# A column sum over 256 MB: eight running rows on VectorE in place of a fold and a TensorE sum for every load

## The chip, the cores and the metric

The kernel runs on one NeuronCore of a Trainium2 chip. A core has TensorE (matrix products, results in PSUM), VectorE (called DVE in a profile), ScalarE (ACT), GpSimd (POOL) and SyncE (SP), each with an instruction queue of its own that is worked off in order. Here SP issues all loads from HBM into SBUF. Every transfer is cut into pieces that 16 DMA engines carry side by side. The engines wait for each other and for transfers through semaphores.

The metric is the time of one execution on the device in microseconds.

## What is computed

```python
def setup_inputs():
    batch, seq, dim = 32, 1024, 2048
    return {"grad_output": np.random.randn(batch, seq, dim).astype(np.float32)}

def reference(grad_output):
    return np.sum(grad_output, axis=(0, 1)).astype(np.float32)
```

The gradient of a bias: 32,768 vectors of 2048 floats are added up to one. That is 268.4 MB read once, and 8 KB written.

## The kernel before

The input is taken as 32,768 lines of 2048 floats. What is called a row below is 128 such lines, one in each of SBUF's 128 partitions: a tile of 128x2048 floats, 1 MB (1,048,576 bytes). There are 256 rows. A load brings several rows at once; those of one partition lie one behind the other in HBM.

**Buffers.** One tile, `ring`, has three slots (`SLOTS`) of eight rows (`M`), 64 KB in each partition. `UNITS` lists the loads: 29 of eight rows, then 6, 4, 3, 3, 3, 2, 2. Unit i goes to slot i % 3. The last two units leave out the last 256 columns (`B`) of their rows, and behind them come one more row without these columns and five small loads of 256 columns, `late`, for the columns left out.

**A unit's way.** SP issues its load (`load`, L113). VectorE waits until it has landed (`take`) and folds it to two rows in place (`fold`, L69): rows 4 to 7 are added to rows 0 to 3, a 128x8192 add, then rows 2 and 3 to rows 0 and 1, a 128x4096 add. TensorE then adds the two rows over the partitions (`sums`, L95): a matmul with a column of ones in place of weights, for four quarters of the 2048 columns in four column groups of the array, summed up in the PSUM tile `acc`. In a profile a row's sums are eight records. When both rows are summed, TensorE raises `s_free`, and SP, which waits for it, issues the load that reuses the slot. So unit i alone decides when load i+3 is issued.

TensorE also computes filler products into the tile `junk` (L158, `FILL` = 3, 0, 2 for the three slots) that nobody reads.

**Order.** All semaphores are written out by hand within `tile_critical`. VectorE's 27 first units are a loop on its own queue (9 rounds of three slots), and TensorE's 36 units are one of 12 rounds.

**The end.** After the last units TensorE sums the late row into `acc` and the five late pieces into a second PSUM tile, `accr` (L174). ScalarE copies `acc` to SBUF (`res`, L188). The second half of the columns lies in two PSUM partitions in alternating blocks of 128; ScalarE and VectorE each put one of them in order (`joint`, L192). VectorE adds `accr` to the last 256 columns (L197). Four stores write the result: SP the first 1024 columns (L201), ScalarE the joint ones (L205), and SP and ScalarE 128 each of the last 256 (L208).

Of the kernel before, what the change touches and what calls it, by code (L numbers as in the profile page):

```python
# [7 lines left out]
P = 128  # L8
M = 8
SLOTS = 3  # L10
LOOPS = 9
UNITS = (M,) * 29 + (6, 4, 3, 3, 3, 2, 2)
B = 256
LATE = 5
FILL = (3, 0, 2)


@with_exitstack
def kernel(
# [10 lines left out]

    nc = tc.nc
    f32 = mybir.dt.float32
    D = out.shape[-1]
    flat = grad_output.rearrange("b s d -> (b s) d")
    Q = D // 4
    H = B // 2
    W = M * D  # L40
    add = mybir.AluOpType.add
    C = D - B

    sb = ctx.enter_context(tc.tile_pool(name="sb", bufs=1))
    ps = ctx.enter_context(tc.tile_pool(name="ps", bufs=1, space=bass.MemoryType.PSUM))
    ring = sb.tile([P, SLOTS * W], f32, name="ring")
    ones = sb.tile([P, 1], f32, name="ones")
    fill = sb.tile([P, 512], f32, name="fill")
    res = sb.tile([P, Q], f32, name="res")
    joint = sb.tile([P, C - 2 * Q], f32, name="joint")  # L50
    acc = ps.tile([P, 512], f32, name="acc")
    accr = ps.tile([P, 512], f32, name="accr")
    junk = ps.tile([P, 512], f32, name="junk")

    some = lambda name, n: [tc.alloc_semaphore(f"{name}{k}") for k in range(n)]
    landed, red, late = some("landed", SLOTS), some("red", SLOTS), some("late", 1 + LATE)
    s_one, s_free, s_vec, s_left, s_right, s_res, s_end, s_last, s_out = (
        tc.alloc_semaphore(n)
        for n in ("one", "free", "vec", "left", "right", "res", "end", "last", "out")
    )  # L60
    q, v, t, a, p = nc.sync, nc.vector, nc.tensor, nc.scalar, nc.gpsimd

    def take(engine, sem, n):
        engine.wait_ge(sem, n)
        engine.sem_inc(sem, -n)  # L65

    def fold(at, n, by):
        part = ring[:, at : at + n * D]
        return v.tensor_tensor(  # L69
            out=part, in0=part, in1=ring[:, at + by * D : at + (by + n) * D], op=add  # L70
        )

    def unit(i):

        s, m = i % SLOTS, UNITS[i]
        at = s * W
        take(v, landed[s], 16)
        steps = {8: ((4, 4), (2, 2)), 6: ((2, 4), (2, 2)), 4: ((2, 2),), 3: ((1, 2),), 2: ()}[m]
        for k, (n, by) in enumerate(steps):
            if k:  # L80
                take(v, s_vec, 1)
            fold(at, n, by).then_inc(red[s] if k + 1 == len(steps) else s_vec, 1)
        if not steps:
            v.sem_inc(red[s], 1)

    def shares(x):


        ends = x[:, 2 * Q :].rearrange("p (b g c) -> p g b c", g=2, c=H)
        return [x[:, :Q], x[:, Q : 2 * Q], ends[:, 0], ends[:, 1]]  # L90

    def sums(at, w=D):
        for g, x in enumerate(shares(ring[:, at : at + w])):
            o = acc[32 * g : 32 * g + 1, : Q if g < 2 else (w - 2 * Q) // 2]
            mm = t.matmul(  # L95
                o if g < 2 else o.rearrange("p (b c) -> p b c", c=H),
                lhsT=ones[:],
                rhs=x,
                start=False,
                stop=False,  # L100
                tile_position=(0, 32 * g),
                skip_group_check=True,
            )
        return mm

    with tc.tile_critical(sync_engine=mybir.EngineType.Pool):

        def load(at, m, row, c0, w, sem):
            part = ring[:, at : at + m * D].rearrange("p (m d) -> p m d", m=m)[:, :, c0 : c0 + w]
            src = flat[row * P : (row + m) * P].rearrange("(p m) d -> p m d", p=P)[:, :, c0 : c0 + w]  # L110
            if w == D:
                part, src = (x.rearrange("p m d -> p (m d)") for x in (part, src))
            q.dma_start(out=part, in_=src).then_inc(sem, 16)  # L113

        row = 0
        for i, m in enumerate(UNITS):
            if i >= SLOTS:
                q.wait_ge(s_free, i - SLOTS + 1)
            load(i % SLOTS * W, m, row, 0, D if i + 2 < len(UNITS) else C, landed[i % SLOTS])
            row += m  # L120

        end = (len(UNITS) - 1) % SLOTS * W
        load(end + 2 * D, 1, row, 0, C, late[0])
        ends = [(end + 3 * D + k * B) for k in range(LATE)]
        row -= LATE - 1
        for at, m in zip(ends[::2], (2, 2, 1)):
            part = flat[row * P : (row + m) * P].rearrange("(p m) d -> p m d", p=P)
            for j in range(m):
                k = ends.index(at) + j
                q.dma_start(  # L130
                    out=ring[:, at + j * B : at + (j + 1) * B], in_=part[:, j, C:]
                ).then_inc(late[1 + k], 16)
            row += m


        v.memset(ones[:], 1.0).then_inc(s_one, 1)  # L136
        v.memset(fill[:], 0.0).then_inc(s_one, 1)  # L137
        v.memset(acc[:], 0.0).then_inc(s_one, 1)  # L138
        v.memset(accr[:], 0.0).then_inc(s_one, 1)  # L139
        with v.Fori(0, LOOPS) as _:  # L140
            for s in range(SLOTS):
                unit(s)
        for i in range(LOOPS * SLOTS, len(UNITS)):
            if i + 2 >= len(UNITS):
                at = i % SLOTS * W
                v.wait_ge(s_free, i - SLOTS + 1)
                v.memset(  # L147
                    ring[:, at : at + 2 * D].rearrange("p (m d) -> p m d", m=2)[:, :, C:], 0.0
                ).then_inc(s_vec, 1)
                take(v, s_vec, 1)  # L150
            unit(i)


        t.wait_ge(s_one, 4)
        with t.Fori(0, len(UNITS) // SLOTS) as _:
            for s in range(SLOTS):
                for _ in range(FILL[s]):
                    t.matmul(  # L158
                        junk[0:1, :],
                        lhsT=ones[:],  # L160
                        rhs=fill[:],
                        start=True,
                        stop=True,
                        tile_position=(0, 0),
                    )
                take(t, red[s], 1)
                sums(s * W)
                sums(s * W + D).then_inc(s_free, 1)
        t.wait_ge(late[0], 16)
        sums(end + 2 * D, C).then_inc(s_left, 1)  # L170
        for k, at in enumerate(ends):
            t.wait_ge(late[1 + k], 16)
            for g in (2, 3):
                mm = t.matmul(  # L174
                    accr[32 * g : 32 * g + 1, :H],
                    lhsT=ones[:],
                    rhs=ring[:, at + (g - 2) * H : at + (g - 1) * H],
                    start=False,
                    stop=False,
                    tile_position=(0, 32 * g),  # L180
                    skip_group_check=True,
                )
        mm.then_inc(s_right, 1)

        a.wait_ge(s_left, 1)
        a.copy(out=res[0:97, :], in_=acc[0:97, :]).then_inc(s_res, 1)  # L188
        left = joint[64:65, :].rearrange("p (b g c) -> p g b c", g=2, c=H)
        for g, copy in enumerate((a.copy, v.tensor_copy)):  # L190
            (a, v)[g].wait_ge(s_res, 1)
            copy(  # L192
                out=left[:, g],
                in_=res[64 + 32 * g : 65 + 32 * g, : Q - H].rearrange("p (b c) -> p b c", c=H),
            ).then_inc(s_end, 1)
        v.wait_ge(s_right, 1)
        v.tensor_tensor(  # L197
            out=res[64:97, Q - H :], in0=res[64:97, Q - H :], in1=accr[64:97, :H], op=add
        ).then_inc(s_last, 1)
        q.wait_ge(s_res, 1)  # L200
        q.dma_start(  # L201
            out=out[: 2 * Q].rearrange("(g c) -> g c", g=2), in_=res[0:33:32, :]
        ).then_inc(s_out, 16)
        a.wait_ge(s_end, 2)
        a.dma_start(out=out[None, 2 * Q : C], in_=joint[64:65, :]).then_inc(s_out, 16)  # L205
        for g, e in enumerate((q, a)):
            e.wait_ge(s_last, 1)
            e.dma_start(  # L208
                out=out[None, C + g * H : C + (g + 1) * H],
                in_=res[64 + 32 * g : 65 + 32 * g, Q - H :],  # L210
            ).then_inc(s_out, 16)
        p.wait_ge(s_out, 64)


# [1 line left out]
_INS = ['grad_output']  # L216
_OUTS = [((2048,), 'float32')]
# [25 lines left out]
```

## Time and profile before

| | us |
|---|---|
| three runs: median (lowest to highest) | 629.33 (629.27 to 629.43) |
| profiled execution, its own time | 629.16 |
| its span, first to last instruction | 627.4 |
| VectorE busy | 403.8 (64%), 72 instructions |
| TensorE busy | 188.6 (30%), 724 records |
| of these the filler products | 72.4, 120 records |
| bytes read | 268.44 MB, 428 GB/s over the span |

The span begins with the first instruction of the kernel and ends with the last; the execution's own time also has what lies before and after. A line of the groups gives the source line, the engine, the operation, what is written from what, the shape, the count; behind the first bar the busy time in all and the mean of one in ns; behind the second the time that the engine stood idle before them and what ended it. A line of the timeline gives start and duration in us. Where it shows several instructions merged, as two adds of a unit, the duration goes from the first start to the last end.

### The profile page before, as it was taken

To read this page: it belongs to the slowest core of one execution; us is meant where nothing else is said; L and a number is where in the kernel's file an instruction comes from. 1 tells how busy PE (TensorE), PEld (TensorE's weight loads), DVE (VectorE), ACT (ScalarE), POOL (GpSimd) and SP (SyncE) were. 2 spreads that over 40 slices of the span, in tenths; PEclk is the share of its full clock that TensorE was granted. 3 is DMA by queue.
4 is the path that set the end of the run, shared out by engine and by line. 5 is a ranking of instruction groups with operands and counts; after the bars stand their busy time and mean duration, and the time that the engine had idled before them with its cause. 6 is when DMAs were issued, how large, how long until landed. Compare 5 with 4: busy or idle time off the path is not lost. (4 is left out here: it accounts for less than half of the span.)

```text
span 627.4 us, 1778 instructions
## 1 busy us (share of the span) xinstructions
PE 188.6 (30%) x724; PEld 29.1 (5%) x724; DVE 403.8 (64%) x72; ACT 2.4 (0%) x3; POOL 0.2 (0%) x4
## 2 busy tenths in 40 slices
PE   3023222342034231323420342214233213421776
PEld 0000000000000000000000000000000000000111
DVE  0566786667866668766687666786666866668732
ACT  0000000000000000000000000000000000000000
POOL 0000000000000000000000000000000000000000
PEclk8565576756577656766566766577665767665879
DMA  9999999999999999999999999999999999999997
GB/s 401 401 468 401 468 401 468 401 468 401 468 401 468 401 464 405 464 405 460 409 455 414 447 422 439 430 430 439 422 447 414 455 409 460 405 447 418 429 422 285
DMA packets 6314, 268.45 MB, mean 428 GB/s; under 512 B 677, under 2 KB 1319, under 8 KB 1962
## 3 DMA queue, kind: packets, MB, share of 16 engines
q1 hardware_dynamic: 6310, 268.44, 99.1%
q10 hardware_dynamic: 4, 0.00, 0.0%
HBM read 268.44 MB, written 0.01 MB: 428 GB/s over the span
## 5 line engine op out<-in xcount | busy, mean ns | idle before, releaser
L69 DVE TENSOR_TENSOR ring<-ring 128x8192 f32<-128x8192 f32 (+2 forms) x64 | 400.5, 6258 | 210.0 <-DVEq L65 205.6
L95 PE MATMUL acc<-ring,ones 128*1 128x512 f32 (+1 forms) x584 | 121.3, 969 | 432.5 <-PEq L65 432.4
L158 PE MATMUL junk<-fill,ones 128*1 128x512 f32 x120 | 72.4, 744 | 2.9 <-DVE accr L139 2.9
L95 PEld LDWEIGHTS acc<-ring,ones 128*1 128x1 f32 x584 | 15.4, 100 | 519.7 <-issue 518.7
L158 PEld LDWEIGHTS junk<-fill,ones 128*1 128x1 f32 x120 | 13.1, 110 | 73.8 <-issue 73.8
L192 DVE COPY joint<-res 1x384 f32<-1x384 f32 x1 | 0.5, 547 | 7.6 <-ACT res L188 7.6
L188 ACT COPY res<-acc 97x512 f32<-97x512 f32 x1 | 0.6, 586 | 620.8 <-PE acc L95 620.8
L147 DVE MEMSET ring<- 128x512 f32 x2 | 1.0, 485 | 1.8 <-PE acc L95 1.8
L174 PE MATMUL accr<-ring,ones 128*1 128x128 f32 x20 | 1.5, 271 | 0.0
L188 ACT ACT_TABLE_LOAD x1 | 1.3, 1283 | 0.9 <-PEq L227 0.9
L136 DVE MEMSET ones<- 128x1 f32 x1 | 0.1, 59 | 1.0 <-PEq L227 1.0
L174 PEld LDWEIGHTS accr<-ring,ones 128*1 128x1 f32 x20 | 0.6, 81 | 1.1 <-DMA ring<-in_grad_output_dram 0.9
L138 DVE MEMSET acc<- 128x512 f32 x1 | 0.5, 485 | 0.1
L137 DVE MEMSET fill<- 128x512 f32 x1 | 0.5, 485 | 0.1
L139 DVE MEMSET accr<- 128x512 f32 x1 | 0.5, 485 | 0.1
L192 ACT COPY joint<-res 1x384 f32<-1x384 f32 x1 | 0.5, 507 | 0.0
L197 DVE TENSOR_TENSOR res<-res,accr 33x128 f32<-33x128 f32 x1 | 0.3, 291 | 0.0
L227 POOL MEMSET const-uint8-127<- 128x1 uint8 x1 | 0.1, 102 | 0.0
L227 POOL MEMSET const-bfloat16-1.0<- 128x1 bf16 x1 | 0.1, 101 | 0.0
L227 POOL MEMSET const-float32-0.0<- 128x1 f32 x1 | 0.1, 99 | 0.2 <-issue 0.2
L227 POOL MEMSET const-float32-1.0<- 128x1 f32 x1 | 0.1, 99 | 0.0
## 6 DMA issues: line engine op xcount, KB each, us to landing
ring<-in_grad_output_dram SPq DMA_DIRECT2D x3, 3072.0 KB, 14.3
ring<-in_grad_output_dram SPq DMA_DIRECT2D x1, 6144.0 KB, 36.0
ring<-in_grad_output_dram SPq DMA_DIRECT2D x1, 4096.0 KB, 26.6
ring<-in_grad_output_dram SPq DMA_DIRECT2D x2, 1792.0 KB, 11.6
ring<-in_grad_output_dram SPq DMA_DIRECT2D x1, 896.0 KB, 11.6
ring<-in_grad_output_dram SPq DMA_DIRECT2D x5, 128.0 KB, 11.1
ring<-in_grad_output_dram SPq DMA_DIRECT2D x29, 40.9
out_dram<-res SPq DMA_DIRECT2D x1, 4.0 KB
```

The costliest lines, as they stand in the source:

```text
L69: return v.tensor_tensor(out=part, in0=part, in1=ring[:, at + by * D : at + (by + n) * D], op=add)
L95: mm = t.matmul(o if g < 2 else o.rearrange("p (b c) -> p b c", c=H), lhsT=ones[:], rhs=x, start=False, stop=False, tile_position=(0, 32 * g),
L137: v.memset(fill[:], 0.0).then_inc(s_one, 1)
L138: v.memset(acc[:], 0.0).then_inc(s_one, 1)
L139: v.memset(accr[:], 0.0).then_inc(s_one, 1)
L147: v.memset(ring[:, at : at + 2 * D].rearrange("p (m d) -> p m d", m=2)[:, :, C:], 0.0).then_inc(s_vec, 1)
L158: t.matmul(junk[0:1, :], lhsT=ones[:], rhs=fill[:], start=True, stop=True, tile_position=(0, 0),)
L174: mm = t.matmul(accr[32 * g : 32 * g + 1, :H], lhsT=ones[:], rhs=ring[:, at + (g - 2) * H : at + (g - 1) * H], start=False, stop=False, ti ...
L188: a.copy(out=res[0:97, :], in_=acc[0:97, :]).then_inc(s_res, 1)
L192: copy(out=left[:, g], in_=res[64 + 32 * g : 65 + 32 * g, : Q - H].rearrange("p (b c) -> p b c", c=H),).then_inc(s_end, 1)
L197: v.tensor_tensor(out=res[64:97, Q - H :], in0=res[64:97, Q - H :], in1=accr[64:97, :H], op=add).then_inc(s_last, 1)
L227: nc = _bacc.Bacc("TRN2", target_bir_lowering=False, num_devices=1)
```

## The change

The hand-written semaphores and the loops go: every instruction is written out in order, under `manual_schedule`, and the framework puts in the waits that the data needs. The ring becomes three tiles.

Of the loads the first 29 (`CHAIN`) are again of eight rows. A load is no longer folded: VectorE adds the buffer of the load before to it, all eight rows in one 128x16384 add (`plus`), so that eight running rows go from buffer to buffer. With the 29th load the chain ends: the eight running rows are folded to one (`fold`, three adds) and this one is added to the first row of load 28. Loads 28, 29 (eight rows) and 30 (seven) are folded to one row each, load 31 (four rows) goes to rows 4 to 7 of load 28's buffer, and three of its rows are put into one by two adds. Then follow a load of two rows and three single rows, without their last 256 columns, into the buffer of load 29, and three small loads of those columns.

TensorE sums ten rows in all, in the order of the list, and the three small pieces. The filler products are gone. At the end GpSimd does the copy that VectorE did, and the last 256 columns go out in one store in place of two.

```diff
-LOOPS = 9
-UNITS = (M,) * 29 + (6, 4, 3, 3, 3, 2, 2)
+CHAIN = 29
 B = 256
-LATE = 5
-FILL = (3, 0, 2)
+LATE = 3
...
-    ring = sb.tile([P, SLOTS * W], f32, name="ring")
+    ring = [sb.tile([P, M * D], f32, name=f"ring{s}") for s in range(SLOTS)]
...
-    def fold(at, n, by):
-        part = ring[:, at : at + n * D]
-        return v.tensor_tensor(
-            out=part, in0=part, in1=ring[:, at + by * D : at + (by + n) * D], op=add
-        )
+    def load(s, at, m):
+        nonlocal row
+        src = flat[row * P : (row + m) * P].rearrange("(p m) d -> p (m d)", p=P)
+        q.dma_start(out=ring[s][:, at * D : (at + m) * D], in_=src)
+        row += m
+    def plus(s, to, n, s2, of):
+        part = ring[s][:, to * D : (to + n) * D]
+        v.tensor_tensor(out=part, in0=part, in1=ring[s2][:, of * D : (of + n) * D], op=add)
+    def fold(s, m, left):
+        while m > left:
+            n = m // 2
+            plus(s, 0, n, s, m - n)
+            m -= n
...
-    with tc.tile_critical(sync_engine=mybir.EngineType.Pool):
...
-        with v.Fori(0, LOOPS) as _:
-            for s in range(SLOTS):
-                unit(s)
...
-        with t.Fori(0, len(UNITS) // SLOTS) as _:
-            for s in range(SLOTS):
-                for _ in range(FILL[s]):
-                    t.matmul(
-                        junk[0:1, :],
...
-                take(t, red[s], 1)
-                sums(s * W)
-                sums(s * W + D).then_inc(s_free, 1)
...
+    with tc.manual_schedule():
+        for i in range(CHAIN):
+            s = i % SLOTS
+            before = (i - 1) % SLOTS
+            load(s, 0, M)
+            if i == 0:
+                v.memset(ones[:], 1.0)
+                v.memset(acc[:], 0.0)
+                v.memset(accr[:], 0.0)
+            elif i < CHAIN - 1:
+                plus(s, 0, M, before, 0)
+            else:
+                fold(before, M, 1)
+                plus(s, 0, 1, before, 0)
+        run, s8, s7 = (s, *((s + k) % SLOTS for k in (1, 2)))
+        load(s8, 0, 8)
+        fold(run, M, 1)
+        load(s7, 0, 7)
+        fold(s8, 8, 1)
+        load(run, 4, 4)
+        fold(s7, 7, 1)
+        plus(run, 4, 1, run, 5)
+        plus(run, 4, 1, run, 6)
+        load(s8, 1, 2)
+        tail = flat[row * P :]
+        for k in range(3):
+            q.dma_start(
+                out=ring[s8][:, (3 + k) * D : (3 + k) * D + C], in_=tail[k * P : (k + 1) * P, :C]
+            )
+        for k in range(LATE):
+            q.dma_start(
+                out=ring[s8][:, 6 * D + k * B : 6 * D + (k + 1) * B],
+                in_=tail[k * P : (k + 1) * P, C:],
+            )
+        sums(run, 7)
+        sums(run, 0)
+        sums(s8, 0)
+        sums(s7, 0)
+        sums(s8, 1)
+        sums(s8, 2)
+        sums(s8, 3, C)
+        sums(s8, 4, C)
+        sums(run, 4)
+        sums(s8, 5, C)
+        for k in range(LATE):
             for g in (2, 3):
...
-        for g, copy in enumerate((a.copy, v.tensor_copy)):
+        for g, copy in enumerate((a.copy, p.tensor_copy)):
...
-        for g, e in enumerate((q, a)):
-            e.wait_ge(s_last, 1)
-            e.dma_start(
-                out=out[None, C + g * H : C + (g + 1) * H],
-                in_=res[64 + 32 * g : 65 + 32 * g, Q - H :],
-            ).then_inc(s_out, 16)
+        q.dma_start(
+            out=out[C:].rearrange("(g c) -> g c", g=2), in_=res[64:97:32, Q - H :]
+        )
```

More of the change, by code (lines that the diff above doesn't have):

```diff
@@ L39 @@
     H = B // 2
-    W = M * D
+    C = D - B
     add = mybir.AluOpType.add
-    C = D - B
     sb = ctx.enter_context(tc.tile_pool(name="sb", bufs=1))
     ps = ctx.enter_context(tc.tile_pool(name="ps", bufs=1, space=bass.MemoryType.PSUM))
-    ring = sb.tile([P, SLOTS * W], f32, name="ring")
+    ring = [sb.tile([P, M * D], f32, name=f"ring{s}") for s in range(SLOTS)]
     ones = sb.tile([P, 1], f32, name="ones")
-    fill = sb.tile([P, 512], f32, name="fill")
     res = sb.tile([P, Q], f32, name="res")
@@ L52 @@
     accr = ps.tile([P, 512], f32, name="accr")
[L53 to L59, printed above, removed]
-    )
-    q, v, t, a, p = nc.sync, nc.vector, nc.tensor, nc.scalar, nc.gpsimd
-    def take(engine, sem, n):
-        engine.wait_ge(sem, n)
-        engine.sem_inc(sem, -n)
-    def fold(at, n, by):
-        part = ring[:, at : at + n * D]
-        return v.tensor_tensor(
-            out=part, in0=part, in1=ring[:, at + by * D : at + (by + n) * D], op=add
[L71 to L84, printed above, removed]
+    q, v, t, a, p = nc.sync, nc.vector, nc.tensor, nc.scalar, nc.gpsimd
+    row = 0
+    def load(s, at, m):
[11 more added lines that the diff above has]
+            m -= n
     def shares(x):
@@ L90, in shares, with sums @@
         return [x[:, :Q], x[:, Q : 2 * Q], ends[:, 0], ends[:, 1]]
-    def sums(at, w=D):
-        for g, x in enumerate(shares(ring[:, at : at + w])):
+    def sums(s, at, w=D):
+        for g, x in enumerate(shares(ring[s][:, at * D : at * D + w])):
             o = acc[32 * g : 32 * g + 1, : Q if g < 2 else (w - 2 * Q) // 2]
-            mm = t.matmul(
+            t.matmul(
                 o if g < 2 else o.rearrange("p (b c) -> p b c", c=H),
@@ L103, in sums @@
             )
-        return mm
-    with tc.tile_critical(sync_engine=mybir.EngineType.Pool):
[L108 to L139, printed above, removed]
-        with v.Fori(0, LOOPS) as _:
-            for s in range(SLOTS):
-                unit(s)
[L143 to L154, printed above, removed]
-        with t.Fori(0, len(UNITS) // SLOTS) as _:
-            for s in range(SLOTS):
-                for _ in range(FILL[s]):
-                    t.matmul(
-                        junk[0:1, :],
[L160 to L165, printed above, removed]
-                take(t, red[s], 1)
-                sums(s * W)
-                sums(s * W + D).then_inc(s_free, 1)
[L169 to L172, printed above, removed]
@@ L173 @@
             for g in (2, 3):
-                mm = t.matmul(
+                x = 6 * D + k * B + (g - 2) * H
+                t.matmul(
                     accr[32 * g : 32 * g + 1, :H],
                     lhsT=ones[:],
-                    rhs=ring[:, at + (g - 2) * H : at + (g - 1) * H],
+                    rhs=ring[s8][:, x : x + H],
                     start=False,
@@ L182 @@
                 )
-        mm.then_inc(s_right, 1)
-        a.wait_ge(s_left, 1)
-        a.copy(out=res[0:97, :], in_=acc[0:97, :]).then_inc(s_res, 1)
+        a.copy(out=res[0:97, :], in_=acc[0:97, :])
         left = joint[64:65, :].rearrange("p (b g c) -> p g b c", g=2, c=H)
-        for g, copy in enumerate((a.copy, v.tensor_copy)):
-            (a, v)[g].wait_ge(s_res, 1)
+        for g, copy in enumerate((a.copy, p.tensor_copy)):
             copy(
@@ L194 @@
                 in_=res[64 + 32 * g : 65 + 32 * g, : Q - H].rearrange("p (b c) -> p b c", c=H),
-            ).then_inc(s_end, 1)
-        v.wait_ge(s_right, 1)
+            )
         v.tensor_tensor(
             out=res[64:97, Q - H :], in0=res[64:97, Q - H :], in1=accr[64:97, :H], op=add
-        ).then_inc(s_last, 1)
-        q.wait_ge(s_res, 1)
+        )
+        q.dma_start(out=out[: 2 * Q].rearrange("(g c) -> g c", g=2), in_=res[0:33:32, :])
+        a.dma_start(out=out[None, 2 * Q : C], in_=joint[64:65, :])
         q.dma_start(
-            out=out[: 2 * Q].rearrange("(g c) -> g c", g=2), in_=res[0:33:32, :]
-        ).then_inc(s_out, 16)
-        a.wait_ge(s_end, 2)
-        a.dma_start(out=out[None, 2 * Q : C], in_=joint[64:65, :]).then_inc(s_out, 16)
-        for g, e in enumerate((q, a)):
-            e.wait_ge(s_last, 1)
-            e.dma_start(
-                out=out[None, C + g * H : C + (g + 1) * H],
-                in_=res[64 + 32 * g : 65 + 32 * g, Q - H :],
-            ).then_inc(s_out, 16)
-        p.wait_ge(s_out, 64)
+            out=out[C:].rearrange("(g c) -> g c", g=2), in_=res[64:97:32, Q - H :]
+        )
 _INS = ['grad_output']
```

## The prediction

> **What bounds the kernel now.** I read the summary page first, then the groups of instructions kept apart by shape, then the timeline, then the stretches at the start, and last the chain of waits. Names as in the sections above: a row is 128x2048 floats (1 MB), a load 8 rows, L*k* the moment VectorE starts on load *k* (0 to 31).
>
> ```profile
> span 627.4 us, 1778 instructions
> DMA  9999999999999999999999999999999999999997
> q1 hardware_dynamic: 6310, 268.44, 99.1%
> ```
>
> The transfers fill the span: 99.1% of it on all 16 DMA engines. Any time in which the DMA queue is empty is added to the end, and so is any work left when the last bytes are in.
>
> ```profile
> L69 DVE TENSOR_TENSOR ring<-ring 128x8192 f32<-128x8192 f32 x29 | 252.1, 8692 | 190.7 <-DVEq L65 190.7
> L69 DVE TENSOR_TENSOR ring<-ring 128x4096 f32<-128x4096 f32 x32 | 141.6, 4424 | 6.4 <-DVEq L65 2.0
> L69 DVE TENSOR_TENSOR ring<-ring 128x2048 f32<-128x2048 f32 x3 | 6.9, 2292 | 12.9 <-DVEq L65 12.9
> ```
>
> The adds lie on a line: (8692 - 4424) / 4096 = 1.042 ns a column, and 8692 - 8192 x 1.042 = 156 ns for each instruction.
>
> ```profile
> 23.03 13.26 DVE L69 TENSOR_TENSOR ring<-ring 128x8192 f32<-128x8192 f32 x2 [20.27 <-DVEq L65]
> 42.35 13.27 DVE L69 TENSOR_TENSOR ring<-ring 128x8192 f32<-128x8192 f32 x2 [6.06 <-DVEq L65]
> 55.77 3.59 PE L95 MATMUL acc<-ring,ones 128*1 128x512 f32 x16 [15.88 <-PEq L65]
> 59.42 0.33 SPq L113 DMA_DIRECT2D ring<-in_grad_output_dram  x1
> 61.70 13.26 DVE L69 TENSOR_TENSOR ring<-ring 128x8192 f32<-128x8192 f32 x2 [6.09 <-DVEq L65]
> 545.47 13.26 DVE L69 TENSOR_TENSOR ring<-ring 128x8192 f32<-128x8192 f32 x2 [6.08 <-DVEq L65]
> ```
>
> L1 to L27 is 503.12 us, so a load takes 503.12 / 26 = 19.35 us, 2.42 us a row. Two adds take 13.26 us; less 8.69 and 4.42 this leaves 0.14 us between dependent adds. A unit is used up alone: adds, 3.59 us of TensorE, and 0.06 us later (59.36 to 59.42) SP issues the load that reuses its buffer. At 59.42 unit 1 is done and load 4 is issued, while load 2 lands at 61.70 and load 3 waits in the queue: a load and a bit of cover, 21.6 us.
>
> ```profile
> 0.90:1.90 1.00, 0.00 (x0) 0.00 (x0) 0.70 (x3) 1.00 (x1) 0.00 (x0) 1.00 0.00 0
> 1.90:2.70 0.80, 0.00 (x0) 0.00 (x0) 0.75 (x2) 0.27 (x1) 0.00 (x0) 1.00 3.89 1311
> ```
>
> Last two columns: DMA share and GB/s, counted where packets start. SP issued the first load at 0.89 (timeline); nothing moves until 1.90. It landed at 23.03, 22.14 us after its issue: 2.79 more than 19.35.
>
> ```profile
> 621.89 1.08 PE acc L95 x4
> 623.00 0.59 ACT res L188
> 623.62 0.55 DVE joint L192
> 624.20 0.29 DVE res L197
> ```
>
> The chain ends: last landing, TensorE's sums until 622.97, copies, stores, 627.4. So 4.43 us follow the sums. The profiled execution took 629.16 us, 1.76 more than its span; the median shown is 629.33, 0.17 above. My sum is made against 629.16.
>
> **The loop.** Removed: per unit two adds, 16 TensorE records and the filler matmuls, all off the path. Added: one 128x16384 add, 8692 + 8192 x 1.042 ns = 17.23 us, under 19.35, so VectorE alone keeps up. But the add of load i+1 also reads load i's buffer. Load i+3 reuses that buffer, so it is now issued at L(i+1) + 17.23 + 0.06 = 17.29 us, with only load i+2 in flight, about 2.06 us before that one lands. The cover falls from 21.6 to 2.06 us. An issue into an empty queue took 22.14 us to land, so L(i+3) is at least L(i+1) + 39.43 if nothing of the 2.79 us overlaps, against 38.70 now. The next load then has more cover, so the loss is 0.73 us for each pair; from L1 to L27 there are 13 pairs: 9.5 us, the upper bound. The lower bound is 0: in the flow DMA engines start on the next load about 0.4 to 1.4 us before the landing is seen (packet starts 524.73 to 525.73, VectorE start 526.13), so descriptors that come 0.7 us after the issue would be just in time. I take a value between: the first issue held SP for 652 ns, the others 328 ns (the source view of that line), so a later issue should be 0.32 us quicker: 39.11 us, 0.41 a pair, 5.3 us.
>
> The Trainium skill, "DMA: Bandwidth & Descriptors", section "Anatomy of one DMA — SWDGE (gpsimd) path", fits a transfer as about 2.0 us fixed plus bytes / 436e9, for the GpSimd path. By it a load would take 21.24 us from issue, the pair 38.53, and the loop would lose nothing: the 641.0 of the first rival. The first load of this trace shows 22.14.
>
> **The tail.** In the built order of the changed kernel VectorE runs, from L27, sixteen adds with no idle time, as every load they need lands earlier: the add of load 27 (16384 columns), its fold to one row (8192, 4096, 2048), 2048 into load 28, then the folds of load 28 and load 29 (14336 each), of load 30 (6144, 4096, 2048), and two of 2048 for load 31. That is 77,824 columns x 1.042 ns = 81.1 us, 16 x 0.156 = 2.5, 15 gaps x 0.144 = 2.2: 85.8 us (the gaps could be 1 us less). From L27 the 32 rows still to land take 77.4 us. So VectorE ends last, which it does not now: the end of the stream no longer covers it. The next-to-last transfers are late as well: the load of two rows into load 29's buffer waits until that fold ends, at 17.23 + 15.8 + 2.4 + 15.8 + 15.8 = 67.1 us after L27, when load 31 is in since 65.3. Behind it on SP stand the six last small loads. Five rows from there: 67.1 + 2.8 + 12.1 = 82.0 us, still under 85.8, so this stall is covered by 3.8 us of VectorE; without that cover it would cost some 5 us.
>
> TensorE is in order too. The sums of load 30's row can start at 80.9 (85.8 less two adds of 2.29 and their gaps), and four more rows' sums stand before the one that waits for VectorE's last add. After a long pause it is slow:
>
> ```profile
> 59.50:60.00 0.50, 0.50 (x2) 0.01 (x1) 0.00 (x0) 0.00 (x0) 0.00 (x0) 0.50 0.00 0
> 60.00:60.50 0.50, 0.50 (x3) 0.14 (x2) 0.00 (x0) 0.00 (x0) 0.00 (x0) 0.91 0.61 262
> 613.42 1.90 PE L95 MATMUL acc<-ring,ones 128*1 128x512 f32 x16 [1.15 <-PEq L65]
> ```
>
> The granted clock (third column from the right) was 0.50 from the burst's start at 55.77 to about 60.05, 4.3 us. Sixteen records are two rows: 3.59 / 2 = 1.79 us a row slow, 1.90 / 2 = 0.95 fast. From 80.9: 4.3 us do 2.4 rows, the other 2.6 of the five take 2.5, end 87.7; two rows after it 1.9: 89.6, so 3.8 us after VectorE. Bounds: 2.0 (all five done in time, two fast rows left) and 7.6 (seven slow rows from 80.9). I take 3.8.
>
> The skill's "TensorE: Matmul & The Clock Gate", section "Part 1: The HAM clock gate", puts the warm-up at one window of about 3.4 us. By that figure the five rows would end 0.4 us earlier, 3.4 in place of 3.8; this trace shows 4.3.
>
> **The end.** GpSimd copies what VectorE copied (0.55 us); ScalarE's second store at 624.83 goes and ScalarE's last store is the one at 624.20. The trace has no GpSimd copy; ScalarE's takes 0.51, VectorE's 0.55, GpSimd's memsets of one column 0.1. Equal to VectorE's, the end comes up to 0.6 us sooner; three times as long, 0.6 later. I take 0.2 less: 4.2 us after the sums (3.8 to 5.0). At the start each engine has one barrier wait fewer: 0 to 0.5 us saved, I take 0.
>
> **Sum:** 545.47 (L27 now) + 5.3 + 85.8 + 3.8 + 4.2 + 1.76 = 646.3 us, slower by 17.
>
> **Rivals.**
> - *The queue never runs dry* (gap 0): descriptors arrive in time behind the load in flight. For: the packet starts above; issue to first packet is partly SP's own time. Against: 22.14 us and the 1.01 us to the first packet. Then 545.47 + 85.8 + 3.8 + 4.2 + 1.76 = 641.0 us.
> - *The whole start of a transfer is exposed*: 0.73 a pair. For: packets of the first wave started at 1.90 and those of the second at 4.80, 2.9 us against 2.42 in the flow. Against: in the loop a load is still moving when the next is issued. 646.3 + 4.2 = 650.5 us.
> - *Not slower: VectorE's adds get faster beside an idle TensorE.* Place: the sixteen adds behind L27. It decides from 0.89 ns a column down: 77,824 x 0.89 = 69.3, with 4.7 fixed 74 us, under the 77.4 of the loads; the 14.7 us add leaves 4.6 us of cover; the end is again the last landing, about 629 us. For: filler and sums share the buffers with the adds. Against: the first pair, at 23.03, ran with TensorE idle and took 13.26 us, the same as all others. If the adds cost what they cost, the end can't come before 545.47 + 85.8 + 2.0 + 3.8 + 1.76 - 0.5 = 638.3.
>
> **How the numbers follow.** Forecast 0.45, no gap 0.25, whole gap 0.25, not slower 0.04, anything else 0.01. The time is the likeliest's, 646.3. Range: the low end is the no-gap case with TensorE's lower bound, 641.0 - 1.8 = 639.2; the high end the whole gap with part of TensorE's upper bound, 650.5 + 1.5 = 652. About 0.2% is what a measurement of this kernel can tell from no change. Slower 0.95, same 0.02, faster 0.03.
>
> **What would show it.** VectorE starts 19.35 to 20.1 us apart in the loop, alternating or about 19.55 even; dips in the packet starts once a load or two; adds of 17.23 us; SP's issues about 2 us before a landing; VectorE busy without a break for 85.8 us from L27; the chain of waits ending in VectorE, TensorE, ScalarE and not in a transfer. I am wrong if the starts stay at 19.35 (then 641), if an add is far from 17.23, or if the last add comes before the last landing.

## The result and the profile after

The changed kernel takes 669.07 us (median of four, 667.20 to 671.01) against 629.3 us: the ratio is 1.0632, with a 95% interval of 1.059 to 1.0674. The prediction said slower, but 646.3 us with 652.0 as the upper end.

The profiled execution took 667.25 us, 21 more than forecast; its parts are compared below. First its page:

```profile
span 665.2 us, 383 instructions
DMA  9999999999999999999999989989999999999983
q1 hardware_dynamic: 5624, 268.44, 95.6%
```

The transfers fill 95.6% of the span in place of 99.1%, and that of a longer span. Only the two last slices and two in the middle show less than 9 tenths, so the rest of the missing share is spread thinly over the run. The wide adds stand in the groups by shape:

```profile
L61 DVE TENSOR_TENSOR ring<-ring,ring 128x16384 f32<-128x16384 f32 x27 | 465.1, 17225 | 124.0 <-DMA ring<-in_grad_output_dram 124.0
```

VectorE's timeline, with one issue of SP, gives start and duration, and in brackets the idle time before and what ended it:

```profile
42.41 17.23 DVE L61 TENSOR_TENSOR ring<-ring,ring 128x16384 f32<-128x16384 f32 x1 [40.42 <-DMA ring<-in_grad_output_dram]
59.66 0.33 SPq L56 DMA_DIRECT2D ring<-in_grad_output_dram  x1
61.75 17.23 DVE L61 TENSOR_TENSOR ring<-ring,ring 128x16384 f32<-128x16384 f32 x1 [2.11 <-DMA ring<-in_grad_output_dram]
84.47 17.23 DVE L61 TENSOR_TENSOR ring<-ring,ring 128x16384 f32<-128x16384 f32 x1 [5.50 <-DMA ring<-in_grad_output_dram]
104.17 17.23 DVE L61 TENSOR_TENSOR ring<-ring,ring 128x16384 f32<-128x16384 f32 x1 [2.48 <-DMA ring<-in_grad_output_dram]
...
573.80 17.23 DVE L61 TENSOR_TENSOR ring<-ring,ring 128x16384 f32<-128x16384 f32 x1 [4.54 <-DMA ring<-in_grad_output_dram]
591.06 15.48 DVE L61 TENSOR_TENSOR ring<-ring 128x8192 f32<-128x8192 f32 x3
606.58 2.29 DVE L61 TENSOR_TENSOR ring<-ring,ring 128x2048 f32<-128x2048 f32 x1
608.90 48.65 DVE L61 TENSOR_TENSOR ring<-ring 128x8192 f32<-128x8192 f32 x11
```

The adds take the 17.23 us that were forecast, and load 3 is issued at 59.66, 2.09 us before load 2 is in. But load 3 then comes 22.72 us after load 2 (61.75 to 84.47), and load 4 19.70 us after that. L27 is at 573.80 where it was at 545.47: 28.3 us are lost in the loop. From there VectorE runs without a break until 657.55, as forecast. The TensorE and ScalarE work that follows, from the same timeline:

```profile
653.08 7.75 PE L78 MATMUL acc<-ring,ones 128*1 128x512 f32 x54 [8.30 <-DVE ring L61]
...
661.34 0.58 ACT L149 COPY res<-acc 97x512 f32<-97x512 f32 x1 [658.52 <-PE accr L137]
```

So the 38.1 us between the two profiled executions (629.16 and 667.25) are 28.3 in the loop and 9.8 behind L27: before, 629.16 - 545.47 = 83.69 us followed L27, now 667.25 - 573.80 = 93.45.

What happens at one issue is seen in stretches counted by packet starts (the last two columns are the DMA share of 16 engines and GB/s). This is the changed kernel at load 3, issued at 59.66:

```profile
59.60:60.50 0.90, 0.00 (x0) 0.00 (x0) 0.04 (x1) 0.00 (x0) 0.00 (x0) 1.00 0.00 0
60.50:62.20 1.70, 0.00 (x0) 0.00 (x0) 0.45 (x1) 0.00 (x0) 0.00 (x0) 1.00 1.62 578
62.20:63.10 0.90, 0.00 (x0) 0.00 (x0) 0.90 (x1) 0.00 (x0) 0.00 (x0) 1.00 0.00 0
63.10:63.30 0.20, 0.00 (x0) 0.00 (x0) 0.20 (x1) 0.00 (x0) 0.00 (x0) 1.00 1.10 328
```

A packet is one partition's 64 KB. 578 GB/s x 1.7 us is 983 KB, 15 packets: fifteen engines begin load 3 between 60.5 and 62.2. 328 GB/s x 0.2 us is one more packet: the sixteenth engine begins at 63.1 to 63.3, 3.5 us after the issue. Its packet takes 1.10 x 0.2 x 16 = 3.5 us, those of the fifteen 1.62 x 1.7 x 16 / 15 = 2.9 on average, a packet in the flow 2.42. The late engine has seven more to do: 63.2 + 3.5 + 7 x 2.42 = 83.6, and the load is seen at 84.47. At this load VectorE waits for the slowest of sixteen engines.

### The profile page after: what moved, and what is told of

Its sections match the earlier page's. It is cut to its first block, busy times and chain, and to the rows that moved or that the text cites. A ratio compares the mean times of both kernels' runs of the same rounds, so it can differ in the third digit from the quotient of the medians.

```text
span 665.2 us, 383 instructions
## 1 busy us (share of the span) xinstructions
PE 12.4 (2%) x92; PEld 2.9 (0%) x92; DVE 532.5 (80%) x46; ACT 2.4 (0%) x3; POOL 0.7 (0%) x5
## 3 DMA queue, kind: packets, MB, share of 16 engines
q1 hardware_dynamic: 5624, 268.44, 95.6%
## 4 chain that ended last, share of the span: by engine, by line
issue 99%; POOLq 0%
POOLq L187 0%; POOLq L176 0%
## 5 line engine op out<-in xcount | busy, mean ns | idle before, releaser
L61 DVE TENSOR_TENSOR ring<-ring,ring 128x16384 f32<-128x16384 f32 (+1 forms) x28 | 467.4, 16692 | 124.0 <-DMA ring<-in_grad_output_dram 124.0
L61 DVE TENSOR_TENSOR ring<-ring 128x2048 f32<-128x2048 f32 (+3 forms) x14 | 63.8, 4576 | 0.4
L78 PE MATMUL acc<-ring,ones 128*1 128x512 f32 (+1 forms) x80 | 12.4, 763 | 648.9 <-DMA ring<-in_grad_output_dram 640.6
L78 PEld LDWEIGHTS acc<-ring,ones 128*1 128x1 f32 x80 | 2.4, 99 | 657.6 <-DVE ring L61 649.8
## 6 DMA issues: line engine op xcount, KB each, us to landing
ring<-in_grad_output_dram SPq DMA_DIRECT2D x1, 7168.0 KB, 21.9
```

What stands on the lines that cost most here:

```text
L61: v.tensor_tensor(out=part, in0=part, in1=ring[s2][:, of * D : (of + n) * D], op=add)
L78: t.matmul(o if g < 2 else o.rearrange("p (b c) -> p b c", c=H), lhsT=ones[:], rhs=x, start=False, stop=False, tile_position=(0, 32 * g), ...
```

## The experiments

The cover is the time for which the transfers already issued still run when SP issues the next load.

**1. The kernel before with a short cover.** One edit: SP waits for one unit more.

```diff
-                q.wait_ge(s_free, i - SLOTS + 1)
+                q.wait_ge(s_free, i - SLOTS + (2 if i < 29 else 1))
```

> The kernel before with one edit: for the 29 loads of eight rows SP waits until unit i-2, not i-3, is summed. The issue then comes some 2.3 us before the load in flight lands, the cover of the changed kernel, with the same adds, sums and filler products as before. Theory (short cover: DMA engines run dry between loads and one of them restarts late): loads about 20.4 us apart in place of 19.35, some 26 x 1.05 = 27 us more, 650 to 660 us. Rival (the wide two-buffer adds or the idle TensorE slow the transfers): nothing changes, 629 us.

Measured 656.84 us, ratio 1.0444 (1.0402 to 1.0486): the theory's number. VectorE's timeline with SP's issue of load 4 (that of load 3 was at 59.10):

```profile
42.21 13.26 DVE L69 TENSOR_TENSOR ring<-ring 128x8192 f32<-128x8192 f32 x2 [6.07 <-DVEq L65]
61.56 13.26 DVE L69 TENSOR_TENSOR ring<-ring 128x8192 f32<-128x8192 f32 x2 [6.09 <-DVEq L65]
78.63 0.33 SPq L113 DMA_DIRECT2D ring<-in_grad_output_dram  x1
82.92 13.26 DVE L69 TENSOR_TENSOR ring<-ring 128x8192 f32<-128x8192 f32 x2 [8.09 <-DVEq L65]
```

Load 3 lands 21.36 us after load 2, though the adds, the sums, the filler and the hand-written waits are those of before. So a loss of 27 us comes from the moment of issue alone; wide adds, an idle TensorE and the framework's waits aren't needed for it.

**2. The changed kernel in halves.**

```diff
-            load(s, 0, M)
+            load(s, 0, 4)
+            load(s, 4, 4)
...
-                plus(s, 0, M, before, 0)
+                plus(s, 0, 4, before, 0)
+                plus(s, 4, 4, before, 4)
```

> The changed kernel, but each of the first 29 loads is issued as two of four rows, and each add of eight rows as two of four. The same columns are added; a half's buffer is free about 20 us before it is needed. Theory (short cover): loads of eight rows 19.35 us apart again, the 28 us of the loop are gone, the tail stays: 638 to 641 us. Rival (VectorE's two-buffer adds slow the transfers): still 665 to 671 us.

Measured 631.9 us, ratio 1.004 (1.0026 to 1.0055): the loss in the loop is gone, and the time is 6 us below the range I expected. The timeline of VectorE's last adds of the loop says why:

```profile
538.61 8.69 DVE L61 TENSOR_TENSOR ring<-ring,ring 128x8192 f32<-128x8192 f32 x1 [1.02 <-DMA ring<-in_grad_output_dram]
548.34 8.69 DVE L61 TENSOR_TENSOR ring<-ring,ring 128x8192 f32<-128x8192 f32 x1 [1.04 <-DMA ring<-in_grad_output_dram]
557.07 15.48 DVE L61 TENSOR_TENSOR ring<-ring 128x8192 f32<-128x8192 f32 x3
```

A half starts when it is in, so only 8.69 us of the running add stand behind the last bytes of load 27, not 17.23. VectorE's work behind L27 then ends at 574.90 + 48.65 = 623.55, before the last sums, which wait for a transfer again (at 625.29 in the timeline, with the last landing as what ended TensorE's idle time). The halves thus cured the tail too, which I hadn't foreseen. What is left over 629.3 fits the loads: they come 9.71 us apart for each half, 19.43 a load, which makes 2 us over the loop.

**3. The cover alone.** Three kernels differ from the changed one only in the wide add's columns (7, 6 and 7.5 of the eight rows), and so in when SP may issue; a fourth adds one row again.

```diff
-                plus(s, 0, M, before, 0)
+                plus(s, 0, 7, before, 0)
```

> The changed kernel with adds over seven of the eight rows (128x14336, 15.1 us) in the loop; the eighth row of most loads is left out of the sum. Cover 4.2 us in place of 2.06. Theory (short cover): most of the 28 us go, loads 19.4 to 19.7 us apart; with 2.1 us less in the tail 637 to 647 us. Rival (load slowed by VectorE's traffic, in proportion): 28 x 7/8 = 25 us remain, 662 us.

Measured 638.29 us (one run). The spacing is the old one, 19.37 on average:

```profile
526.23 15.09 DVE L61 TENSOR_TENSOR ring<-ring,ring 128x14336 f32<-128x14336 f32 x1 [4.25 <-DMA ring<-in_grad_output_dram]
545.59 15.09 DVE L61 TENSOR_TENSOR ring<-ring,ring 128x14336 f32<-128x14336 f32 x1 [4.27 <-DMA ring<-in_grad_output_dram]
560.72 15.48 DVE L61 TENSOR_TENSOR ring<-ring 128x8192 f32<-128x8192 f32 x3
```

> The changed kernel with adds over six of the eight rows (128x12288, 13.0 us) in the loop; two rows of most loads are left out of the sum. Cover 6.3 us. Theory (short cover): all of the 28 us go, loads 19.35 us apart, and the tail is 4.3 us shorter: 633 to 637 us. Rival (in proportion to VectorE's traffic): 21 us remain, 656 us.

Measured 634.69 us (one run): spacing 19.35, as the theory said.

> The changed kernel with adds over 15360 of the 16384 columns in the loop (half a row of most loads is left out of the sum): cover 3.1 us, between the 2.06 that loses a microsecond a load and the 4.2 that loses nothing. Theory (an engine must get its next descriptors before its last 64 KB packet, 2.42 us, has begun, about a microsecond after the issue): needed cover about 3.4 us, so a part of the loss is left, 640 to 655 us. Rival (only the packets' first start counts, 1.0 us): nothing is left, 637 to 639 us.

Measured 660.73 us (one run), beyond both: with 3.2 us of cover little is gained, the spacing is 20.20.

```diff
                 plus(s, 0, M, before, 0)
+                plus(s, 0, 1, before, 0)
```

> The changed kernel with one more add of 2048 columns behind each wide add (the first row of the load before is counted twice), so that a load is issued 19.6 us after the landing before: the queue is then empty, cover -0.2 us. If a load into an empty queue takes 22.14 us as the first one does, two loads take 41.7 us, 20.9 a load, and the time is 678 to 683 us. If the 23.6 us from issue to landing of the changed kernel hold here as well, 21.6 a load and about 700 us.

Measured 678.48 us (one run), the first case. Load 3 is issued at 61.65, when nothing moves any more, and all engines start within 0.9 us of each other. Its stretches by packet starts:

```profile
61.60:62.50 0.90, 0.00 (x0) 0.00 (x0) 0.87 (x2) 0.00 (x0) 0.00 (x0) 1.00 0.00 0
62.50:63.40 0.90, 0.00 (x0) 0.00 (x0) 0.90 (x1) 0.00 (x0) 0.00 (x0) 1.00 3.35 1165
63.40:65.40 2.00, 0.00 (x0) 0.00 (x0) 2.00 (x1) 0.00 (x0) 0.00 (x0) 1.00 0.00 0
```

1165 GB/s x 0.9 us is 16 packets, the last at most 1.75 us after the issue. There is no straggler here, and this load, issued later than load 3 of the changed kernel, takes less time: 21.84 us (to 83.49 in VectorE's starts) where that one took 24.81.

The runs can be compared by their means. If a load is issued a us after a landing and takes x from issue to landing, two loads take a + x, so on average x = 2 T - a, with T the mean spacing from L1 to L27. The cover in the table is that of a load whose forerunner comes on time:

| kernel | a | cover 19.35 - a | T | x |
|---|---|---|---|---|
| one more add (empty queue) | 19.58 | -0.2 | 20.82 | 22.1 |
| changed kernel | 17.25 | 2.1 | 20.44 | 23.6 |
| kernel before, short cover | 17.07 | 2.3 | 20.36 | 23.7 |
| 7.5 rows | 16.18 | 3.2 | 20.20 | 24.2 |
| 7 rows | 15.11 | 4.2 | 19.37 | (23.6, waits in the queue) |
| 6 rows | 13.0 | 6.4 | 19.35 | (25.7, waits in the queue) |

On average a load of the three kernels with covers of 2.1 to 3.2 us needs 23.6 to 24.2 us from its issue. By these means nothing is lost only if the cover is above x - 19.35, about 4.2 to 4.9 us.

The single loads behind the means are unlike, and VectorE's starts in the timelines show it. In the changed kernel 16 of the loads 3 to 27 were issued with less than 3 us of the load ahead still to come: eight of them were in after 21.9 to 22.6 us and lost at most 0.7, five took 24.4 to 25.0 and lost 2.4 to 3.4. So the long start comes irregularly. In the run with one more add eight loads were issued into silence or nearly so (at most 0.2 us still to come) and took 21.7 to 22.5 us; 13 others had 1.5 to 2.9 us of cover, and eleven of these took no more than 22.5 us either. Why short cover costs so little there and so much in the changed kernel stays open.

**4. Is it the size of the packets?** Loads in pieces of 16 KB:

```diff
-        src = flat[row * P : (row + m) * P].rearrange("(p m) d -> p (m d)", p=P)
-        q.dma_start(out=ring[s][:, at * D : (at + m) * D], in_=src)
+        b = 2 if m == M else m
+        src = flat[row * P : (row + m) * P].rearrange("(n p b) d -> p n (b d)", p=P, b=b)
+        to = ring[s][:, at * D : (at + m) * D].rearrange("p (n x) -> p n x", x=b * D)
+        q.dma_start(out=to, in_=src)
```

> The changed kernel with the loads of eight rows in pieces of 16 KB of one partition in place of 64 KB; the same bytes, adds and waits, cover 2.06 us. Theory (the last packet of an engine has to be still to come when the next descriptors arrive): a packet now takes 0.6 us in place of 2.42, so 2.06 us are enough, loads 19.4 to 19.6 us apart, 639 to 645 us. Rival (an engine restarts late whatever the packets are): no change, 660 to 671 us.

Measured 672.76 us (two runs), ratio 1.0694 (1.0661 to 1.0728): a little beyond even the rival's range. The theory of the 64 KB packet fell; T is 20.57.

**5. Is it the one queue?** Every second load from ScalarE's queue:

```diff
-            load(s, 0, M)
+            load(s, 0, M, q if i % 2 == 0 else a)
```

> The changed kernel with every second of the first 29 loads issued by ScalarE's queue in place of SP's; same loads, adds and waits, cover 2.06 us. The runs so far fit one law: from issue to landing a load takes 22.1 us alone but about 23.6 when it is issued beside a load that is still moving. If the later start belongs to the one queue (descriptors stand behind those in flight), the other queue's start is hidden: 637 to 645 us. If it comes from the traffic on the DMA engines whichever queue issues: 658 to 672 us.

Measured 677.16 us (one run): slower than either case, T 20.87. A second queue doesn't help, but the run doesn't decide between the two cases, because the loads now come in another pattern. From load 7 on VectorE waits some 7 us before every second add (starts 210.19, 251.73, 293.32) and not at all before the one behind it. The load seen at 251.73 was issued by ScalarE at 227.44, when the load ahead was already in; sixteen packets began between 228.3 and 229.3, so no engine was late, and it still took 24.3 us. Meanwhile SP had issued the next load at 244.70. That the two loads then hold each other up on the engines is likely, but not shown.

So why an engine begins late beside traffic stays open. It is not the size of the packets; whether it belongs to SP's queue isn't settled.

**6. Versions without both losses.** VectorE keeps seven running rows, TensorE sums the eighth of each load; after 25 loads the rest goes as in the kernel before.

```diff
-CHAIN = 29
+CHAIN = 25
+UNITS = (8, 6, 4, 3, 3, 3, 2, 2)
...
-                plus(s, 0, M, before, 0)
+                plus(s, 0, 7, before, 0)
+            sums(s, 7)
...
+        units = (8, 8, 8) + UNITS
+        for j, m in enumerate(units):
+            s = (run + 1 + j) % SLOTS
+            last = j + 2 >= len(units)
+            for n, by in steps[m]:
+                plus(s, 0, n, s, by)
+            for k in range(2):
+                sums(s, k, C if last else D)
...
```

> A version meant to have neither loss: seven running rows on VectorE (adds of 14336 columns, cover 4.2 us), the eighth row of each load summed by TensorE; after 25 loads the running rows are folded to two and the rest goes as in the kernel before, with folds, TensorE and small last loads, but without filler products and with the end of the changed kernel. Theory: loads 19.35 us apart, the end bound by the last landing as before: 628.0 to 630.5 us, 0.2% either way of the kernel before. If wide adds or the framework's waits cost something by themselves: over 633 us.

Measured 635.68 us, ratio 1.0103 (1.0085 to 1.012): over 633, so by its number the second case. The loss is in the loop: single loads still come 0.1 to 1.0 us late, and from L1 to L24 the mean spacing is 19.56, which makes 4.8 us. A cover of 4.2 us is the edge.

> As the version with seven running rows, but six on VectorE (12288 columns, 13.0 us) and two rows of each load summed by TensorE: cover 6.3 us in place of 4.2, at which the version with seven still lost some 5 us. Theory (issue to landing about 23.6 to 24.2 us beside traffic, so a cover of 5 us is enough): loads 19.35 us apart throughout, 628.0 to 630.0 us. If the losses of the version with seven came from TensorE reading beside the landing: 634 us or more.

Measured 630.58 us, ratio 1.0019 (1.001 to 1.0028): spacing 19.35 but for one load 1.4 us late (119.57 to 140.35 in VectorE's starts), and the end is bound by the last landing as before. Wide adds and the framework's waits thus cost next to nothing by themselves, nor does TensorE's reading at this cover. Whether TensorE's reading adds to the loss at the edge isn't settled: the 7 rows of experiment 3 had the same cover of 4.2 us without it, and 19.37 (one run). No version tried is quicker than the kernel before.

## Why the prediction was wrong, step by step

The sum had 545.47 + 5.3 + 85.8 + 3.8 + 4.2 + 1.76; the profile has 545.47 + 28.33 + 83.75 + 3.73 + 3.92 + 2.05 = 667.25.

- *The loop's loss (the 5.3): wrong by 23 us, and with it the whole miss.* The mechanism was right: the buffer of load i is also read by the next add, so the next issue comes two microseconds before the queue is empty, and two loads take issue delay plus issue to landing. The step that failed is the bound "at least L(i+1) + 39.43 if nothing of the 2.79 us overlaps", taken as the worst case. I held that a load issued beside another can't take longer to start than the first load of all, 22.14 us. On average it takes 23.6, in the changed kernel and in experiment 1: 17.25 + 23.63 = 40.88 a pair, 2.18 over 38.70, and 13 pairs make the 28.3. Nor did a load behind a late one come in time, as the sum took for granted: four such loads with 4.8 to 5.5 us of cover lost another 0.3 to 0.8 us. VectorE's starts are irregular, 19.3 to 22.7 us apart, and not alternating or even. The rival with the whole start exposed, 650.5 us, had the same fault, so the range ended too early.
- *The value within the bounds*, 0.32 us less because later issues hold SP for less time, fits a load issued into silence: 21.84 us for load 3 of the run with one more add, 0.30 less than 22.14. But the loads of the changed kernel are issued beside one that is still moving, where the bound itself didn't hold.
- *The Trainium skill's fit* ("DMA: Bandwidth & Descriptors", "Anatomy of one DMA — SWDGE (gpsimd) path") of about 2.0 us fixed, given there for the GpSimd path, would have had no loss in the loop. The loads here are SP's, and the runs show 22.14 - 19.35 = 2.79 us for the first load and on average 23.6 - 19.35 = 4.3 in the changed kernel. The measurements decide against using it here.
- *VectorE's tail: right, 2 us too long.* It took 83.75 us for 85.8; the gaps between dependent adds were 0.02 to 0.03 us under the framework's waits, not 0.144.
- *The stall of the late two-row load: there, and covered, as forecast.* It was issued at 639.80, 66.0 us after L27 (67.1 forecast). The last of the small loads was issued at 642.8 and took 12.3 us to land, so the last landing was near 655.1, 81.3 us after L27 (82.0 forecast) and 2.4 us ahead of VectorE's end at 657.55 (3.8 forecast).
- *TensorE's slow start: right.* The granted clock was 0.50 from the burst's start at 653.08 to about 657.2 (4.1 us, 4.3 forecast), and the sums ended 3.7 us after VectorE (3.8).
- *The end: right.* GpSimd's copy took 0.50 us, 3.9 us of span followed the sums (4.2 forecast), and 2.05 lay around the span where 1.76 did.
- *Not slower because VectorE gets faster:* no; with TensorE idle the wide add took 17.225 us, what the rows of before gave.

## What to carry to other kernels

When a stream of loads is the bound, find for every load which instruction releases its buffer, and count how much is still in the queue at that moment: an add that reads two buffers releases the older one a whole load later than a fold that reads its own. Keep enough transfers queued: for the 8 MB loads of these runs 6.4 us cost nearly nothing, 4.2 were the edge, and 2.1 cost 1.1 us for every load on average. The first load's time into an empty queue isn't an upper bound for a load issued beside others.

## What had not been expected of the hardware

A load issued while another one is still moving can start later on some DMA engines than one issued into silence. At load 3 engines began 0.9 to 3.5 us after the issue in the changed kernel, and 0.9 to 1.75 in the run with one more add; in the changed kernel the first packets took 2.9 us on average on fifteen engines and 3.5 on the late one, where 2.42 is usual. This doesn't happen at every load, but often enough to make a cover of 2 to 3 us worth little: 3.2 us of cover (20.20 us a load) save only 0.6 us a load against the run with one more add (20.82).
